# A hybrid two-layer trunk on one core: the causal mask moved into the scan, and elementwise steps of the attention half moved to GpSimd in quarter pieces

## The chip, the core and the metric

The kernel runs on one core of one Trainium2 chip. The metric is the device time in microseconds of one execution. The engines are TensorE (PE, with its weight loads as PEld), VectorE (DVE), ScalarE (ACT), GpSimd (POOL) and SyncE (SP, which issues most DMAs). Each engine runs its own instructions in order; they wait for each other through semaphores.

## The reference

All is float32; x is 2048 x 1024. Layer 0 is a pooling mixer, layer 1 a strictly causal stick-breaking attention over 16 heads of 64, with keys and values computed once between them:

```python
for i in range(DEPTH):                       # DEPTH = 2
    if i < N_A:                              # layer 0
        h = rms_norm(x, a_norm[i])
        x = x + pool_mixer(h, a_w_in[i], a_w_group[i], a_scale[i], a_w_out[i])
    else:                                    # layer 1
        k_all, v_all = jnp.split(rms_norm(x, kv_norm) @ w_kv, 2, axis=-1)
        k_sh, v_sh = rms_norm(split_heads(k_all), k_norm), split_heads(v_all)
        q, z = jnp.split(rms_norm(x, b_norm[j]) @ b_w_in[j], 2, axis=-1)
        q = rms_norm(split_heads(q), b_q_norm[j])
        o = stick_breaking_attention(q, k_sh, v_sh)
        x = x + (o * jax.nn.silu(z)) @ b_w_out[j]
    x = x + (p[i] @ ple_w[i]) * jax.nn.sigmoid(x @ ple_gate_w[i])

# attention: A[t,s] = beta[t,s] * prod_{s<j<t} (1 - beta[t,j]), beta = sigmoid(q.k / sqrt(d))
mask = s_idx < t_idx
log_keep = jnp.where(mask, jax.nn.log_sigmoid(-logits), 0.0)
later = lax.cumsum(log_keep, axis=log_keep.ndim - 1, reverse=True) - log_keep
a = jnp.where(mask, jnp.exp(jax.nn.log_sigmoid(logits) + later), 0.0)
out = a @ v
```

## The kernel before

The sequence is cut into four chunks of 512 rows (`W5`). Every float32 operand of a product is held as a pair, its high part and its low part (`pr[:, 0]`, `pr[:, 1]`), and a product is three matmuls: high x high, high x low, low x high. A layout with features on the partitions is used all through; a transpose is a matmul with the identity.

The first half of the program (a list of steps per chunk) computes layer 0, its embedding add and q, k and v, and leaves them in DRAM. The change touches there only the pool of the `halo` tiles.

The second half is the attention. Its main loop runs over passes n. A slot is a head h of query chunk c against key chunk kc (kc from c down to 0), and each slot has four passes, one for each block of 128 queries. Query chunks run from 3 to 0, so chunk 3 has 256 passes, chunk 2 192, chunk 1 128 and chunk 0 64. One pass issues, in this order:

- `turn` for the pass six earlier (L809 to L813): up to four transposes into a PSUM tile `psa` (two buffers), an ACT copy into the high part of `at` (L812), and a DVE subtraction for the low part (L813), which frees `psa`.
- `front` (L784 to L795): two matmuls make the logits in `psl` (two buffers), ACT writes `kap` = sigmoid(-logits) (L788, four tiles). In the diagonal slot (kc == c) a GpSimd select (L790) puts 1 wherever the key is not before the query in the last 128 columns. Then DVE scans backwards, a running product (multiply by `kap`, add zero), with the result of the slot before as the initial value (L795). Attention weights are differences of neighbouring running products; the differences are taken on v instead, in the first half.
- a number of filler matmuls: the generator `filler` yields after each matmul, and `rate` says how many a pass takes.
- `gather` for the pass eight earlier (L821, L822): two matmuls with `at` into `pso`. At the end of a head the two halves of `pso` are summed into `os` (ACT copy L826, DVE add L827). After every second head, four ACT instructions add a bias per query block (L833) and GpSimd multiplies by the gate of z (L834).

The filler of chunk 3 is `gate_z` (L883 to L886): for each of the four chunks, the product of z, the norm (a DVE multiply that reads PSUM), the sigmoid on ACT and the multiply on GpSimd, and a store. The filler of chunk c < 3 is `post(c+1)`: output projection and residual add (L907), the pair of the result `x3` (ACT cast L909, GpSimd subtraction L910), the gate product and its sigmoid (L929), the embedding product, a DVE multiply (L932), two last adds of the low and the high part of `x3` (L933 on GpSimd, on DVE in the tail; L934 on DVE), and in `finish` four transposes, an ACT copy into `ot` (one buffer) and the store (L939 to L942). `pair_up` makes the pair of an `os` (ACT cast L862, DVE subtraction L863). `post(0)` is the tail, after the loop; there `tail[0]` is set.

The order of instructions on each engine follows the order in which they are issued, with a scheduler that may move an instruction by a few places. What is left of a filler when a chunk of queries ends is issued at once; `rate` is the filler's number of steps over the passes that are to take it.

Of the kernel before, what the change touches and what calls it, by code (L numbers as in the profile page):

```python
# [8 lines left out]
F32 = mybir.dt.float32  # L9
# [25 lines left out]
def trunk_kernel(ctx, tc, x, p, a_norm, a_w_in, a_w_group, a_scale, a_w_out, kv_norm, w_kv,  # L35
# [143 lines left out]
    with ExitStack() as st:  # L179
# [17 lines left out]
        halo = [[cp.tile([P, HALO], F32, name=f"halo{o}_{i}") for i in range(2)] for o in range(KT)]  # L197
# [549 lines left out]
    with ExitStack() as st:  # L747
# [10 lines left out]
        V.memset(zeros, 0.0)  # L758
        kcount = [0]
# [17 lines left out]
        def front(st, j):  # L777

            w = (j + 1) * P if st["diag"] else W5
            r0 = W5 - w  # L780
            ps = psl.tile([P, W5], F32, tag="psl", name="psl")
            qs = slice(j * P, (j + 1) * P)
            (qa, qb), kk = st["q"], st["k"]
            T.matmul(ps[:, :w], qa[:, qs], kk[:, :w], start=True, stop=False)  # L784
            T.matmul(ps[:, :w], qb[:, qs], kk[:, :w], start=False, stop=True)  # L785
            kp = kaps[kcount[0] % NK]
            kcount[0] += 1
            A.activation(out=kp[:, r0:], in_=ps[:, :w], func=AF.Sigmoid, scale=-1.0)  # L788
            if st["diag"]:
                G.affine_select(out=kp[:, W5 - P :], in_=kp[:, W5 - P :], pattern=[[-1, P]], compare_op=ALU.is_gt,  # L790
                                fill=1.0, base=0, channel_multiplier=1)

            def scan():
                pp = ppool.tile([P, W5], F32, tag="pp", name="pp")
                V.tensor_tensor_scan(out=pp[:, r0:][:, ::-1], data0=kp[:, r0:][:, ::-1],  # L795
                                     data1=zeros.to_broadcast([P, w]),
                                     initial=1.0 if st["diag"] else st["carry"][j], op0=ALU.mult, op1=ALU.add)
                st["carry"][j] = pp[:, r0 : r0 + 1]
                st["a"].append((pp, r0))

            return scan
# [14 lines left out]
        def gather(st, kt):  # L816
# [6 lines left out]
            if st["last"] and kt == 3:  # L823
                half, os, c, h2 = st["h"] % 2, st["os"], st["c"], st["h"] // 2
                mine, other = slice(half * HD, (half + 1) * HD), slice((1 - half) * HD, (2 - half) * HD)
                A.copy(out=os[mine], in_=po[other])  # L826
                V.tensor_tensor(out=os[mine], in0=po[mine], in1=os[mine], op=ALU.add)  # L827
                if half:
# [5 lines left out]
                    G.tensor_tensor(out=os, in0=os, in1=zt, op=ALU.mult)  # L834
                    outs[c].append(os)

        tail = [0]
# [19 lines left out]
        def pair_up(c):  # L857

            if len(ogs[c]) < len(outs[c]):
# [3 lines left out]
                V.tensor_tensor(out=pr[:, 1], in0=os, in1=f(pr[:, 0]), op=ALU.subtract)  # L863
                ogs[c].append(pr)

        def gate_z(c):
# [11 lines left out]
            for o in range(KT):  # L878
# [4 lines left out]
                V.tensor_tensor(out=zr, in0=ps, in1=rb, op=ALU.mult)  # L883
                sg = t2.tile([P, W5], F32, tag="tmp", name="sgz", bufs=4)
                A.activation(out=sg, in_=zr, func=AF.Sigmoid)
                G.tensor_tensor(out=zr, in0=zr, in1=sg, op=ALU.mult)  # L886
# [5 lines left out]
        POST = 8 * 24 + 8 * 30 + 9  # L892

        def post(c):

            pin = t2.tile([P, 4, PLE], F32, tag="pin", name="pin", bufs=1)
# [4 lines left out]
            for o in range(KT):  # L901
# [8 lines left out]
                G.tensor_tensor(out=pr[:, 1], in0=xr, in1=f(pr[:, 0]), op=ALU.subtract)  # L910
# [12 lines left out]
            for o in range(KT):  # L923
                wg = stored(wgd[o])
                wl = stored(wld[o])
                ps = dense()
# [6 lines left out]
                (V if tail[0] else G).tensor_tensor(out=sg, in0=sg, in1=f(x3[o][:, 1]), op=ALU.add)  # L933
                V.tensor_tensor(out=sg, in0=sg, in1=f(x3[o][:, 0]), op=ALU.add)  # L934
# [14 lines left out]
                if c:  # L949
                    pair_up(c - 1)  # L950
                yield
# [25 lines left out]
        def begin(i):  # L977
            c, h, kc = slots[i]
            if kc == c:
                if h == 1:  # L980
                    early["ends"] = load_ends(c)
                os = head["os"] if h % 2 else t2.tile([P, W5], F32, tag="os", name="os", bufs=9)
                head.clear()
                head.update(q=early.pop("q", None) or load_q(c, h), carry=[None] * 4, o=[], os=os)
# [3 lines left out]
        for n in range(4 * len(slots) + LAG_G):  # L988
# [70 lines left out]
```

## Time and profile before

| | |
|---|---|
| time, median of 3 runs | 2778.84 us (2777.24 to 2779.99) |
| time of the profiled execution | 2781.82 us |
| its span, first to last instruction | 2779.0 us |
| PE busy | 2729.7 us (98%) |
| DVE busy | 1950.7 us (70%) |
| ACT busy | 1390.0 us (50%) |
| POOL busy | 956.8 us (34%) |
| DMA | 573.28 MB, mean 206 GB/s |
| mean granted TensorE clock | 0.999 |

The span ends some 3 us below the time of the same execution; what lies around it does not depend on the kernel's work. A row of a group names the source line, the engine, the operation, output <- inputs, the shape, the count, then busy us and mean ns of one, then the engine's idle time in front of it and what ended that. A row of the waits says who waited for whom: total us, times, longest. PE's matmuls overlap and their ends are modelled, so a busy PE isn't PE at its peak.

### The profile page before, as it was taken

What the parts mean: (1) busy time and instruction counts of PE and PEld (TensorE: products, weight loads), DVE (VectorE), ACT (ScalarE), POOL (GpSimd) and SP (SyncE); (2) the same over time, 40 slices, a digit from 0 to 9 for tenths busy, and PEclk for the clock granted to TensorE, in tenths of its full rate; (3) what the DMA queues carried; (4) which work ended last, traced back from release to release, by engine and by line L of the source; (5) the groups of instructions that cost most, each with busy time, mean ns of one, the idle gap of its engine ahead of it and who ended that gap; (6) DMA issues with size and microseconds to landing.
All of it is one profiled execution on the core that took longest, in us unless ns stands there. A gap on an engine that the chain in (4) does not pass through costs nothing. (4 is left out here: it accounts for less than half of the span.)

```text
span 2779.0 us, 40467 instructions
## 1 busy us (share of the span) xinstructions
PE 2729.7 (98%) x13715; PEld 2261.3 (81%) x13715; DVE 1950.7 (70%) x2573; ACT 1390.0 (50%) x2801; POOL 956.8 (34%) x949
## 2 busy tenths in 40 slices
PE   9999999999999999999999999999999999999999
PEld 7888888888888888888878888887878778878877
DVE  6667535655357544575499999999999988886642
ACT  5445532545234542345355566666666655564431
POOL 2575338642475425753211211121111122213220
PEclk9999999999999999999999999999999999999999
DMA  8655695737946488445688565555455655658765
GB/s 283 240 190 178 219 328 197 234 136 259 350 138 236 154 260 304 137 143 178 189 247 283 176 216 171 163 171 184 157 166 170 183 183 183 196 183 265 240 202 161
DMA packets 335844, 573.28 MB, mean 206 GB/s; under 512 B 32463, under 2 KB 166639, under 8 KB 335637
## 3 DMA queue, kind: packets, MB, share of 16 engines
q1 hardware_dynamic: 330186, 563.03, 62.3%
q10 hardware_dynamic: 5450, 7.66, 0.9%
q8 instruction: 108, 1.77, 0.3%
q14 instruction: 100, 0.81, 0.1%
HBM read 430.01 MB, written 132.19 MB: 202 GB/s over the span
## 5 line engine op out<-in xcount | busy, mean ns | idle before, releaser
L535 PE MATMUL psd<-wpair,x 128*128 128x512 f32 x2304 | 543.8, 393 | 0.0
L812 ACT CAST at<-psa 128x512 fp32r<-128x512 f32 (+3 forms) x640 | 333.4, 522 | 395.4 <-PE psa L809 389.4
L795 DVE TENSOR_TENSOR_SCAN pp<-kap,pp,zeros 128x512 f32<-128x512 f32 x384 | 507.6, 1323 | 6.2 <-ACT kap L788 4.8
L535 PEld LDWEIGHTS psd<-wpair,x 128*128 128x128 f32 x2304 | 428.1, 188 | 86.2
L813 DVE TENSOR_TENSOR at<-psa,at 128x512 fp32r<-128x512 f32 (+3 forms) x640 | 378.9, 594 | 58.1 <-ACT at L812 55.7
L809 PE MATMUL psa<-ident,pp 128*128 128x128 f32 x2176 | 346.4, 275 | 21.6 <-DVE at L813 17.7
L788 ACT ACTIVATE kap<-psl 128x512 f32<-128x512 f32 (+3 forms) x640 | 343.9, 538 | 18.9 <-PE psl L785 16.3
L809 PEld LDWEIGHTS psa<-ident,pp 128*128 128x128 f32 x2176 | 263.4, 140 | 99.4 <-DVE at L813 41.7
L790 POOL TENSOR_SCALAR_AFFINE_SELECT kap<-kap 128x128 f32<-128x128 f32 x256 | 93.2, 365 | 557.9 <-ACT kap L788 525.3
L784 PE MATMUL psl<-kk,qa 128*128 128x512 f32 (+3 forms) x640 | 280.6, 438 | 1.5 <-DMA kk<-kd 0.8
L795 DVE TENSOR_TENSOR_SCAN pp<-kap,zeros 128x128 f32<-128x128 f32 (+3 forms) x256 | 215.6, 842 | 43.3 <-POOL kap L790 39.6
L821 PE MATMUL pso<-at,vv 128*128 128x512 f32 (+3 forms) x640 | 234.5, 366 | 1.3 <-ACT at L812 1.2
L822 PE MATMUL pso<-at,vv 128*128 128x512 f32 (+3 forms) x640 | 235.4, 368 | 0.0
L785 PE MATMUL psl<-kk,qb 128*128 128x512 f32 (+3 forms) x640 | 234.1, 366 | 0.0
L131 PE MATMUL psd<-xp,wpair 128*128 128x512 f32 x512 | 202.0, 396 | 1.8 <-ACT xp L268 1.3
L132 PE MATMUL psd<-xp,wpair 128*128 128x512 f32 x512 | 200.7, 392 | 0.0
L133 PE MATMUL psd<-xp,wpair 128*128 128x512 f32 x512 | 200.1, 391 | 0.0
L113 DVE SCALAR_TENSOR_TENSOR wpair<-wraw,gains,wpair 128x512 fp32r<-128x512 f32 x192 | 170.6, 909 | 36.6 <-ACT wpair L112 33.2
L108 POOL TENSOR_TENSOR wpair<-wraw,wpair 128x512 fp32r<-128x512 f32 x99 | 144.4, 1475 | 60.4 <-ACT wpair L106 60.4
L112 ACT ACTIVATE wpair<-wraw,gains 128x512 fp32r<-128x512 f32 x192 | 135.0, 719 | 56.1 <-PE psd L535 32.0
L821 PEld LDWEIGHTS pso<-at,vv 128*128 128x128 f32 x640 | 120.4, 188 | 28.0 <-ACT at L812 2.3
L822 PEld LDWEIGHTS pso<-at,vv 128*128 128x128 f32 x640 | 120.4, 188 | 24.8
(210 smaller groups left out, 5453.9 us busy)
## 6 DMA issues: line engine op xcount, KB each, us to landing
kk<-kd SPq DMA_DIRECT2D x320, 128.0 KB
vv<-vd SPq DMA_DIRECT2D x160, 256.0 KB
wraw<-in_w_kv_dram SPq DMA_DIRECT2D x128, 256.0 KB
wpair<-wzd SPq DMA_DIRECT2D x64, 512.0 KB
wpair<-wod SPq DMA_DIRECT2D x64, 512.0 KB
wpair<-wgd SPq DMA_DIRECT2D x64, 512.0 KB
wpair<-wu SPq DMA_DIRECT2D x48, 512.0 KB
wpair<-wi SPq DMA_DIRECT2D x36, 512.0 KB
```

The source lines that it names most:

```text
L131: T.matmul(ps, wst(units, kt, 0, c0), acts[kt][:, 0], start=(begin and kt == order[0]), stop=False)
L132: T.matmul(ps, wst(units, kt, 0, c0), acts[kt][:, 1], start=False, stop=False)
L535: T.matmul(pss2[i], ck["x2"][kt][:, xh, tk], wst(ws, kt, wh, 0, W5), start=(kt == 0 and xh == 0 and wh == 0), stop=(kt == KT - 1 and wh == 1))
L784: T.matmul(ps[:, :w], qa[:, qs], kk[:, :w], start=True, stop=False)
L785: T.matmul(ps[:, :w], qb[:, qs], kk[:, :w], start=False, stop=True)
L788: A.activation(out=kp[:, r0:], in_=ps[:, :w], func=AF.Sigmoid, scale=-1.0)
L795: V.tensor_tensor_scan(out=pp[:, r0:][:, ::-1], data0=kp[:, r0:][:, ::-1], data1=zeros.to_broadcast([P, w]), initial=1.0 if st["diag"] els ...
L809: T.transpose(pt[:, j * P : (j + 1) * P], pp[:, r0 + kt * P : r0 + (kt + 1) * P], ident)
L812: A.copy(out=at[:, 0, cs], in_=pt[:, cs])
L813: V.tensor_tensor(out=at[:, 1, cs], in0=pt[:, cs], in1=f(at[:, 0, cs]), op=ALU.subtract)
L821: T.matmul(po[:, cs], vv[:, kt, :], at[:, 0, cs], start=(st["diag"] and kt == 0), stop=False)
L822: T.matmul(po[:, cs], vv[:, kt, :], at[:, 1, cs], start=False, stop=(st["last"] and kt == 3))
```

## The change

- The mask. A tile `ahead`, zero but for ones where the key is not before the query in the last 128 columns, is made once on GpSimd. In a diagonal slot the scan multiplies by `kap` and takes the maximum with `ahead`, and the select of `kap` on GpSimd is gone. Other slots scan as before.
- `pooled` runs an elementwise operation on GpSimd in four pieces of 128 columns; for the last pair of heads of chunk 0 and in the tail it is one DVE instruction.
- The head sum: ACT copies one half of `pso` into a new tile `low` and the other into `os`, and the sum is `pooled`. The multiply by the gate, the low part of an `os` (L863), the low part of `x3` and the two multiplies on z are `pooled` as well; for the norm of z ACT first copies the PSUM tile.
- The last sums: `xw`, the sum of both parts of `x3`, is made ahead of the gate product (`pooled`), and one add (`pooled`; DVE in the tail) takes the place of two.
- The filler of chunks 2 to 0 is spread over 64c - 4 passes in place of 64c - 16, and the last `finish` of a `post` is held back six steps (so `POST` is 448 and not 441).
- `halo` moves to a pool that ends with the first half, and `pin` is taken from the ring of pairs (18 buffers), which makes room for `ahead` and `low`.

```diff
@@ front
-            if st["diag"]:
-                G.affine_select(out=kp[:, W5 - P :], in_=kp[:, W5 - P :], pattern=[[-1, P]], compare_op=ALU.is_gt,
-                                fill=1.0, base=0, channel_multiplier=1)
...
-                V.tensor_tensor_scan(out=pp[:, r0:][:, ::-1], data0=kp[:, r0:][:, ::-1],
-                                     data1=zeros.to_broadcast([P, w]),
-                                     initial=1.0 if st["diag"] else st["carry"][j], op0=ALU.mult, op1=ALU.add)
+                if st["diag"]:
+                    V.tensor_tensor_scan(out=pp[:, r0:][:, ::-1], data0=kp[:, r0:][:, ::-1],
+                                         data1=ahead[:, r0:][:, ::-1], initial=1.0, op0=ALU.mult, op1=ALU.max)
+                else:
+                    V.tensor_tensor_scan(out=pp[:, ::-1], data0=kp[:, ::-1], data1=zeros.to_broadcast([P, W5]),
+                                         initial=st["carry"][j], op0=ALU.mult, op1=ALU.add)
@@ gather
-                A.copy(out=os[mine], in_=po[other])
-                V.tensor_tensor(out=os[mine], in0=po[mine], in1=os[mine], op=ALU.add)
+                low = st["low"]
+                last[0] = c == 0 and h2 == NH // 2 - 1
+                A.copy(out=low[mine], in_=po[other])
+                A.copy(out=os[mine], in_=po[mine])
+                pooled(os[mine], os[mine], low[mine], ALU.add)
...
-                    G.tensor_tensor(out=os, in0=os, in1=zt, op=ALU.mult)
+                    pooled(os, os, zt, ALU.mult)
+        def pooled(out, in0, in1, op):
+            if tail[0] or last[0]:
+                V.tensor_tensor(out=out, in0=in0, in1=in1, op=op)
+                return
+            for j in range(4):
+                js = slice(j * P, (j + 1) * P)
+                G.tensor_tensor(out=out[:, js], in0=in0[:, js], in1=in1[:, js], op=op)
@@ pair_up
-                V.tensor_tensor(out=pr[:, 1], in0=os, in1=f(pr[:, 0]), op=ALU.subtract)
+                pooled(pr[:, 1], os, f(pr[:, 0]), ALU.subtract)
@@ gate_z
-                V.tensor_tensor(out=zr, in0=ps, in1=rb, op=ALU.mult)
+                A.copy(out=zr, in_=ps)
+                pooled(zr, zr, rb, ALU.mult)
...
-                G.tensor_tensor(out=zr, in0=zr, in1=sg, op=ALU.mult)
+                pooled(zr, zr, sg, ALU.mult)
@@ post
-        POST = 8 * 24 + 8 * 30 + 9
+        POST = 8 * 24 + 8 * 31 + 8
...
-            pin = t2.tile([P, 4, PLE], F32, tag="pin", name="pin", bufs=1)
+            pin = f(pair("pin")).rearrange("q e (j n) -> q (e j) n", n=PLE)
...
-                G.tensor_tensor(out=pr[:, 1], in0=xr, in1=f(pr[:, 0]), op=ALU.subtract)
+                pooled(pr[:, 1], xr, f(pr[:, 0]), ALU.subtract)
...
+                xw = t2.tile([P, W5], F32, tag="tmp", name="xw", bufs=4)
+                pooled(xw, f(x3[o][:, 0]), f(x3[o][:, 1]), ALU.add)
...
-                (V if tail[0] else G).tensor_tensor(out=sg, in0=sg, in1=f(x3[o][:, 1]), op=ALU.add)
-                V.tensor_tensor(out=sg, in0=sg, in1=f(x3[o][:, 0]), op=ALU.add)
+                if tail[0]:
+                    V.tensor_tensor(out=sg, in0=sg, in1=xw, op=ALU.add)
+                else:
+                    pooled(sg, sg, xw, ALU.add)
...
+            for _ in range(6):
+                yield
             late.pop()()
@@ main loop
-                            rate = POST / (64.0 * c3 - 2 * LAG_G)
+                            rate = POST / (64.0 * c3 - 4)
```

More of the change, by code (lines that the diff above doesn't have):

```diff
@@ L195, in tmp @@
             return t2.tile([P, W5], F32, tag="tmp", name=nm, bufs=8)
-        halo = [[cp.tile([P, HALO], F32, name=f"halo{o}_{i}") for i in range(2)] for o in range(KT)]
+        hp = st.enter_context(tc.tile_pool(name="hp", bufs=1))
+        halo = [[hp.tile([P, HALO], F32, name=f"halo{o}_{i}") for i in range(2)] for o in range(KT)]
         for o in range(KT):
@@ L758, in trunk_kernel @@
         V.memset(zeros, 0.0)
+        ahead = kap.tile([P, W5], F32, name="ahead")
+        G.memset(ahead, 0.0)
+        G.affine_select(out=ahead[:, W5 - P :], in_=ahead[:, W5 - P :], pattern=[[-1, P]], compare_op=ALU.is_gt,
+                        fill=1.0, base=0, channel_multiplier=1)
         kcount = [0]
@@ L982, in begin @@
                 os = head["os"] if h % 2 else t2.tile([P, W5], F32, tag="os", name="os", bufs=9)
+                low = head["low"] if h % 2 else t2.tile([P, W5], F32, tag="low", name="low", bufs=1)
                 head.clear()
[L984 removed]
+                head.update(q=early.pop("q", None) or load_q(c, h), carry=[None] * 4, o=[], os=os, low=low)
             kk = early["k"].pop(0) if early["k"] else load_k(kc, h)
```

2 lines of the change are left out of this document (1 added, 1 removed).

## The prediction

> **What bounds the kernel now.** I read the page's busy times first, then the windows of the attention half cut at the four query chunks, then the waits of PE, DVE and ACT there, then groups and the timeline of single passes.
>
> ```profile
> PE 2729.7 (98%) x13715; PEld 2261.3 (81%) x13715; DVE 1950.7 (70%) x2573; ACT 1390.0 (50%) x2801; POOL 956.8 (34%) x949
> ```
>
> TensorE (PE) is nearly full over the whole span, VectorE (DVE) and the others are not. The windows below are chunks 3, 2, 1, 0 of the queries and the tail; the columns are length, busy time of PE, PE's weight loads, DVE, ACT and POOL, then clock and DMA.
>
> ```profile
> 1367.00:1868.00 501.00, 495.58 (x2695) 412.81 (x2694) 469.71 (x563) 299.54 (x597) 97.08 (x106) 1.00 0.65 204
> 1868.00:2225.00 357.00, 345.49 (x1919) 283.04 (x1917) 343.05 (x434) 227.83 (x468) 62.97 (x89) 1.00 0.55 172
> 2225.00:2488.00 263.00, 254.03 (x1399) 211.10 (x1399) 231.31 (x303) 157.23 (x337) 58.28 (x88) 1.00 0.60 188
> 2488.00:2662.00 174.00, 168.89 (x900) 141.90 (x901) 112.61 (x180) 87.28 (x206) 51.86 (x87) 0.99 0.77 247
> 2662.00:2779.00 117.00, 109.33 (x510) 88.93 (x508) 32.10 (x49) 24.01 (x47) 13.61 (x11) 0.98 0.52 167
> ```
>
> Length less PE busy is PE's idle time: 5.4, 11.5, 9.0, 5.1 and 7.7 us, together 38.7 us. The change issues the same matmuls, so this is the most that it can give back, though PE's ends are modelled and some waiting may hide in its busy time. DVE is at 94% and 96% in chunks 3 and 2, so there the two engines are close to a tie. The waits from 1367 to 2662 (total us, times, longest) say what holds DVE, and through it PE:
>
> ```profile
> PE psa L809 <- DVE at L813: 17.7, 33, 1.4
> ```
>
> ```profile
> DVE at L813 <- ACT at L812: 54.4, 113, 1.9
> DVE pp L795 <- POOL kap L790: 39.6, 62, 1.9
> DVE sg L934 <- POOL sg L933: 21.5, 18, 1.4
> ```
>
> ```profile
> ACT og L862 <- POOL os L834: 16.7, 15, 1.8
> ACT sgz L885 <- DVE zr L883: 13.4, 17, 2.6
> ```
>
> PE's largest wait is for DVE's subtraction, which frees the PSUM tile of the transposes; DVE itself waits 39.6 us for the mask on POOL and 21.5 us for the first of the two last sums.
>
> **The change part by part.** These are the groups in the same window (mean ns after the busy time):
>
> ```profile
> L795 DVE TENSOR_TENSOR_SCAN pp<-kap,pp,zeros 128x512 f32<-128x512 f32 x384 | 507.6, 1323 | 6.2 <-ACT kap L788 4.8
> L813 DVE TENSOR_TENSOR at<-psa,at 128x512 fp32r<-128x512 f32 x446 | 299.5, 672 | 35.3 <-ACT at L812 34.1
> ...
> L827 DVE TENSOR_TENSOR os<-pso,os 64x512 f32<-64x512 f32 x61 | 41.5, 680 | 4.9 <-ACT os L826 3.9
> ...
> L883 DVE TENSOR_TENSOR zr<-psd,rb 128x512 f32<-128x512 f32 x32 | 21.3, 667 | 0.4 <-PE psd L854 0.4
> L863 DVE TENSOR_TENSOR og<-os,og 128x512 fp32r<-128x512 f32 x30 | 21.3, 716 | 5.2 <-ACT og L862 5.2
> L934 DVE TENSOR_TENSOR sg<-sg,x 128x512 f32<-128x512 f32 x24 | 20.3, 846 | 21.5 <-POOL sg L933 21.5
> ```
>
> ```profile
> L790 POOL TENSOR_SCALAR_AFFINE_SELECT kap<-kap 128x128 f32<-128x128 f32 x256 | 93.2, 365 | 557.9 <-ACT kap L788 525.3 <-DVE pp L795 18.7 <-DVE at L813 8.9
> L886 POOL TENSOR_TENSOR zr<-zr,sgz 128x512 f32<-128x512 f32 x32 | 60.3, 1884 | 212.6 <-issue 136.7 <-ACT sgz L885 44.1 <-DVE at L813 19.5
> ```
>
> *DVE.* Head sums 62 x 0.680 = 42 us, norm of z 32 x 0.667 = 21, low parts of heads 31 x 0.716 = 22, last sums 24 x 0.846 = 20: 105 us of work leave DVE. The waits for the mask (39.6) and for POOL's half of the last sum (21.5) go too, 166 us in all out of the 1157 us that DVE is busy in the four chunks. What is late next behind the mask is the sigmoid on ACT, which the scan then waits for directly; behind the last sums it is nothing, since DVE no longer touches them.
>
> *The scan of the diagonal blocks* multiplies and takes the maximum instead of adding. No row shows that form; the nearest is the scan that adds, 1.323 us at full width. I have no reason for either sign, so I allow 3% both ways: 256 scans of at most 1.323 us make that at most 10 us of DVE time, inside the relief below, and I take 0. Making the `ahead` tile adds a memset and one select (nearest row 0.365 us) in front of the first scan, where four extra filler matmuls a pass cover it; uncovered it costs under 1 us.
>
> *POOL* loses 256 selects and runs some 260 operations in four pieces. The length of a piece is bounded by the select, 0.365, and by half of this one with 256 columns:
>
> ```profile
> L215 POOL TENSOR_TENSOR kpair<-kraw,kpair 128x256 fp32r<-128x256 f32 x8 | 6.4, 798 | 29.4 <-ACT kpair L214 29.4
> ```
>
> I take 0.40 us. What such pieces do to DVE is seen where a multiplication meets a scan, and the same rows give a pass of chunk 3:
>
> ```profile
> 1608.73 0.61 ACT L788 ACTIVATE kap<-psl 128x512 f32<-128x512 f32 x1
> ...
> 1609.47 1.28 DVE L795 TENSOR_TENSOR_SCAN pp<-kap,pp,zeros 128x512 f32<-128x512 f32 x1
> 1610.03 0.59 ACT L812 CAST at<-psa 128x512 fp32r<-128x512 f32 x1 [0.70 <-PE psa L809]
> 1610.51 0.60 ACT L788 ACTIVATE kap<-psl 128x512 f32<-128x512 f32 x1
> ...
> 1611.84 1.28 DVE L795 TENSOR_TENSOR_SCAN pp<-kap,pp,zeros 128x512 f32<-128x512 f32 x1
> ...
> 1612.13 2.08 POOL L886 TENSOR_TENSOR zr<-zr,sgz 128x512 f32<-128x512 f32 x1 [15.03 <-issue]
> ...
> 1613.35 0.69 DVE L813 TENSOR_TENSOR at<-psa,at 128x512 fp32r<-128x512 f32 x1 [0.23 <-ACT at L812]
> ...
> 1616.15 0.60 PE L809 MATMUL psa<-ident,pp 128*128 128x128 f32 x4
> ```
>
> The multiplication began 0.29 us into a scan and ended 1.09 us after it: it stood still for most of the scan, and ran beside the subtraction, which reads PSUM. So pieces run in the 0.69 us of a subtraction: two of 0.40 overrun it by 0.1, a burst of four needs two gaps and costs the scans some 0.2 us. 260 bursts x 0.2 = 52 us, if a scan gets its turn between pieces. That leaves 166 - 52 = 114 us of relief.
>
> The Trainium skill, in "SBUF — State Buffer", section "Who interferes with whom", says that a DVE instruction with two SBUF inputs and a GpSimd instruction that reads SBUF exclude one another for a whole instruction. By that rule a burst is delayed as in these rows, which agree with it.
>
> *ACT.* It gets 64 more copies of half heads and 32 of z. At the 0.59 us of the `at` copy in these rows that is 57 us; ACT is busy 300 of 501 us in chunk 3, so the time is there, and its order is the question. The changed program puts, in 18 of 32 cases, on ACT: copy of z, one `at` copy, sigmoid of z, sigmoid `kap`; in most others `kap` stands one place earlier. The sigmoid of z now waits for four POOL pieces, and `kap` or the next `at` is queued behind it, with DVE's scan and subtraction waiting for those. Worked on the pass above: `kap` ends at 1609.34, the copy of z fits into the 0.70 us hole, the scan bars POOL until 1610.75, four pieces end near 1612.35, the sigmoid (0.63) near 1613.0, `kap` near 1613.5 instead of 1611.11. The scan is late by 2.0 to 2.4 us. PE stands this for about 2.1 us: the subtraction that ended at 1614.04 freed the tile that the transposes took at 1616.15. So a z costs PE between 0 and 0.9 us (pieces of 0.365 or 0.47, scan early or late); I take 0.35, 32 x 0.35 = 11 us, and as DVE's backlog there otherwise goes (most of the 5.4 us), chunk 3 becomes 6 us longer. Before, DVE did this multiplication in 0.67 us and ACT lost 13.4 us in all.
>
> *Chunk 2.* Relief: 16 x 0.680 + 8 x 0.716 + 8 x 0.846 = 23 us, and about 10 + 7 of the two waits, against some 56 bursts x 0.2 = 11. DVE falls 29 us clear of PE, but eight pairs of heads make ACT wait for POOL (the 16.7 us row shows it now). Of 11.5 us idle I take 7 back.
>
> *Chunks 1 and 0.* The filler is now spread over 64c-4 passes instead of 64c-16. With c = 1, 441 steps in 48 passes become 448 in 60. Before, the last 16 passes of a chunk had no filler, and PE went at DVE's pace, 1.323 + 0.672 = 2.0 us a full pass. Of 9.0 and 5.1 us idle I take back 7 and 2.5.
>
> *Tail.* One sum fewer behind the last product:
>
> ```profile
> 2773.16 0.69 DVE L934 TENSOR_TENSOR sg<-sg,x 128x512 f32<-128x512 f32 x1
> ...
> 2775.12 0.59 ACT L941 COPY ot<-psao 128x512 f32<-128x512 f32 x1 [2.41 <-DMA out_dram<-ot]
> ```
>
> The last copy waits for the DMA of the tile before it, not for the sum, so the 0.69 us are hidden. I take 0. The first half of the program keeps its order. `pin` moves to another pool; its load is still issued eight products ahead of its use, cost 0.
>
> **Sum:** +6 - 7 - 7 - 2.5 = -10.5 us. The profiled execution took 2781.82 us, 3 above the median of 2778.84, so -10.5 against the median: 2768.
>
> **Rivals.**
> 1. *Slower: ACT's queue.* If the sigmoid of z runs more than 0.65 us later than worked above (each piece delayed by a scan of its own, or head sums queued behind z on POOL), every z costs PE 1.0 us: 32 - 5 = +27, and the pairs of heads halve the other gains to -8: +19, 2798. For it: ACT already waits in order for POOL and DVE (16.7 and 13.4 us). Against: DVE's lighter load lets it catch up between two z. It decides from a scan 2.1 us late on.
> 2. *No difference.* PE is the bound, chunk 3 loses about what chunks 2 to 0 win: 2777.
> 3. *Slower: the pieces hold the scans.* If each of the 640 scans waits for one piece, 640 x 0.40 = 256 us exceed the relief of 166 by 90, while DVE's free time in chunks 3 to 1 is 31 + 14 + 32 us; some 30 us come through, 2809. The Trainium skill, "Perfetto Trace Analysis", section "Optimizing Scalar/DVE Operations", warns that moving work between DVE and GpSimd might not help because they share a read port. Against: two pieces fit beside a subtraction.
>
> **How the numbers follow.** Forecast 0.50, rival 1 0.30, rival 2 0.12, rival 3 0.08. Both signs hold much, so the forecast's own range is 2750 to 2773: at best chunk 3 loses nothing and three quarters of the 38.7 us come back. The whole range takes in rivals 1 and 2, with 5 us for what the two prices of a piece leave open beyond rival 1 and 6 below for waiting hidden in PE's busy time: 2744 to 2803. About 0.2% (5.6 us) can be told from no change: faster 0.50, same 0.12, slower 0.38.
>
> **What would show it.** Right: PE's wait for the subtraction under 10 us in chunks 2 to 0, no DVE wait for POOL, DVE busy some 60 to 100 us less, and in chunk 3 a new ACT wait, sigmoid of z for POOL, of 1 to 2 us each. Rival 1: chunk 3 longer than 515 us. Rival 3: mean scan above 1.45 us. Wrong altogether: chunk 3 shorter than 495 us, or chunks 2 to 0 not shorter.

## The result, and the profile after

The changed kernel took 2815.65 us (median of 4 runs, 2814.37 to 2819.01) against 2778.04 for the kernel before beside it: a ratio of 1.0139, 95% interval 1.0126 to 1.0152. The forecast was 2768, the range 2744 to 2803; the time lies above both. The profiled execution took 2814.37 us, its span is 2812.5. From the page, section 1:

```profile
PE 2739.1 (97%) x13715; PEld 2266.9 (81%) x13715; DVE 1879.9 (67%) x2433; ACT 1435.8 (51%) x2897; POOL 1337.5 (48%) x1615
```

DVE has 71 us less work, as forecast (60 to 100), and the span is 33.5 us longer. So DVE's load did not decide. The same windows as before, cut at the chunks:

```profile
1366.00:1898.00 532.00, 503.82 (x2695) 413.37 (x2695) 438.77 (x510) 319.11 (x643) 254.09 (x369) 1.00 0.61 192
1898.00:2265.00 367.00, 347.17 (x1914) 285.72 (x1913) 332.20 (x402) 234.56 (x484) 157.80 (x228) 0.99 0.52 162
2265.00:2522.00 257.00, 252.23 (x1398) 210.73 (x1397) 214.10 (x275) 165.62 (x352) 130.17 (x220) 1.00 0.65 194
2522.00:2687.00 165.00, 162.18 (x881) 137.76 (x879) 101.96 (x147) 95.15 (x220) 111.72 (x212) 0.99 0.79 246
2687.00:2812.50 125.50, 117.03 (x537) 95.12 (x535) 35.70 (x54) 26.82 (x51) 8.00 (x17) 0.98 0.58 186
```

Chunk 3 grew by 31 us, chunk 2 by 9 to 10. Length less PE busy is 28.2, 19.8, 4.8, 2.8 and 8.5 us: PE idles 64.1 us where it idled 38.7, and is busy 9.1 us longer with the same matmuls (the last section shows where from). The last two windows must be read together: 881 and 537 matmuls stand where 900 and 510 stood, so filler went from chunk 0 into the tail. The waits from 1366 to 2687 say who waits:

```profile
DVE at L819 <- ACT at L818: 180.1, 235, 3.5
ACT sgz L905 <- POOL zr L854: 55.3, 30, 4.4
PE psa L815 <- DVE at L819: 35.4, 43, 3.4
DVE pp L802 <- ACT kap L794: 29.4, 32, 2.7
ACT os L842 <- POOL os L854: 23.6, 26, 2.5
ACT og L881 <- POOL os L854: 19.5, 16, 2.5
```

ACT now waits 98 us for GpSimd, in three places. Behind it DVE's wait for the high part of `at` rose from 54.4 to 180.1 us and PE's wait for the subtraction from 17.7 to 35.4. Of the two, PE's is the one to go by: the experiments will show DVE waiting nearly as long in a run that is 50 us faster. The timeline shows one such wait (start, length, then engine, line and tile; the bracket is the idle time before it):

```profile
1457.60 1.38 POOL L854 TENSOR_TENSOR os<-os,zt 128x128 f32<-128x128 f32 x1
...
1458.94 2.65 POOL L854 TENSOR_TENSOR zr<-zr,rb 128x128 f32<-128x128 f32 x4
1459.22 1.27 DVE L802 TENSOR_TENSOR_SCAN pp<-kap,pp,zeros 128x512 f32<-128x512 f32 x1
1459.36 0.66 PE L815 MATMUL psa<-ident,pp 128*128 128x128 f32 x4 [0.15 <-DVE at L819]
...
1460.08 0.39 PE L791 MATMUL psl<-kk,qb 128*128 128x512 f32 x1
...
1461.62 0.63 ACT L905 ACTIVATE sgz<-zr 128x512 f32<-128x512 f32 x1 [2.82 <-POOL zr L854]
1462.16 0.57 ACT L818 CAST at<-psa 128x512 fp32r<-128x512 f32 x1
...
1462.62 0.60 ACT L794 ACTIVATE kap<-psl 128x512 f32<-128x512 f32 x1
1462.76 0.69 DVE L819 TENSOR_TENSOR at<-psa,at 128x512 fp32r<-128x512 f32 x1 [2.27 <-ACT at L818]
...
1463.37 1.32 DVE L802 TENSOR_TENSOR_SCAN pp<-kap,pp,zeros 128x512 f32<-128x512 f32 x1
1463.50 0.66 PE L815 MATMUL psa<-ident,pp 128*128 128x128 f32 x4 [1.87 <-DVE at L819]
```

Four pieces of the norm of z took 2.65 us, as a scan came between them. They began only when GpSimd was done with the last piece of a gate's product, 1.1 us after ACT's copy of z had ended (at 1457.82). So the sigmoid of z stood at the head of ACT's queue for 2.82 us. Behind it stood the copy `at` of a transpose that PE had finished at 1460.02, and the sigmoid `kap` of logits finished at 1460.47. DVE had nothing for 2.27 us, and PE, whose PSUM tile DVE frees, for 1.87 us. This is one of the longer of these waits; 30 of them come to 55.3 us, 1.8 us each.

### The profile page after: what moved, and what is told of

The parts are those of the page before. It is cut to its first block, busy times and chain, and to the rows that moved or that the text cites. A ratio compares the mean times of both kernels' runs of the same rounds, so it can differ in the third digit from the quotient of the medians.

```text
span 2812.5 us, 40373 instructions
## 1 busy us (share of the span) xinstructions
PE 2739.1 (97%) x13715; PEld 2266.9 (81%) x13715; DVE 1879.9 (67%) x2433; ACT 1435.8 (51%) x2897; POOL 1337.5 (48%) x1615
## 5 line engine op out<-in xcount | busy, mean ns | idle before, releaser
L802 DVE TENSOR_TENSOR_SCAN pp<-kap,pp,zeros 128x512 f32<-128x512 f32 x384 | 510.6, 1330 | 31.4 <-ACT kap L794 29.4
L815 PE MATMUL psa<-ident,pp 128*128 128x128 f32 x2176 | 348.3, 275 | 43.3 <-DVE at L819 35.4
L854 POOL TENSOR_TENSOR os<-os,low 64x128 f32<-64x128 f32 x248 | 154.4, 651 | 236.9 <-ACT os L835 234.8
L799 DVE TENSOR_TENSOR_SCAN pp<-kap,ahead 128x128 f32<-128x128 f32 (+3 forms) x256 | 232.6, 909 | 18.1 <-ACT kap L794 16.8
L854 POOL TENSOR_TENSOR zr<-zr,rb 128x128 f32<-128x128 f32 x128 | 81.5, 665 | 204.7 <-ACT zr L902 204.7
L827 PEld LDWEIGHTS pso<-at,vv 128*128 128x128 f32 x640 | 120.7, 189 | 27.5 <-ACT at L818 0.5
```

Of the source, the lines that this page charges most:

```text
L802: V.tensor_tensor_scan(out=pp[:, ::-1], data0=kp[:, ::-1], data1=zeros.to_broadcast([P, W5]), initial=st["carry"][j], op0=ALU.mult, op1=AL ...
L815: T.transpose(pt[:, j * P : (j + 1) * P], pp[:, r0 + kt * P : r0 + (kt + 1) * P], ident)
L827: T.matmul(po[:, cs], vv[:, kt, :], at[:, 0, cs], start=(st["diag"] and kt == 0), stop=False)
L854: G.tensor_tensor(out=out[:, js], in0=in0[:, js], in1=in1[:, js], op=op)
```

## Experiments

Chunk lengths in this part run from the first sigmoid `kap` of one chunk to that of the next, in the profiled execution. "Theory Q" is the prediction's rival 1 taken further: the price is ACT waiting in order for GpSimd. "Theory P" is its rival 3: the pieces' own load on the port and on DVE. Each group of runs has its own runs of the kernel before; their medians went from 2778.1 to 2779.9. The first half of the program, which the edits leave as it is, ended 1364 to 1370 us into the profiled executions, so a few us between two runs can lie outside the attention.

**Two ways to take ACT's wait for z away.** First, issue the sigmoid later, all work staying on GpSimd:

```diff
-                sg = t2.tile([P, W5], F32, tag="tmp", name="sgz", bufs=4)
-                A.activation(out=sg, in_=zr, func=AF.Sigmoid)
-                pooled(zr, zr, sg, ALU.mult)
-                nc.sync.dma_start(out=zd[c][o], in_=zr)
+                zlate.append(silu)      # the four lines, issued nine filler steps on
```

> The changed kernel, with the same instructions, but the sigmoid of z and what follows it is issued nine filler steps (three to four passes) later, so that ScalarE does not reach it before GpSimd's four pieces are done. Theory Q (ScalarE's queue: sigmoid of z stands in front of the next kap and at copies while it waits for GpSimd): chunk 3 gives back about 25 of the 31 us that it lost, 2788 us (2780 to 2796), and the wait of the sigmoid of z for GpSimd, 55 us, falls under 5. Theory P (the pieces hold the scans through the shared port): the same pieces run, 2812 to 2818 us.

Second, the norm of z back on DVE:

```diff
-                A.copy(out=zr, in_=ps)
-                pooled(zr, zr, rb, ALU.mult)
+                V.tensor_tensor(out=zr, in0=ps, in1=rb, op=ALU.mult)
```

> The changed kernel with the norm of z back on VectorE, one instruction that reads PSUM, as before the change; nothing else. Theory Q: about 2790 us (2782 to 2798); VectorE gets 21 us of work back, ScalarE waits under 15 us for the norm. Theory P: 32 of some 260 bursts are gone, an eighth of the 37 us: 2811 us.

Measured: 2793.76 us (ratio to the kernel before 1.0049, 1.0034 to 1.0064) and 2794.37 (1.0053, 1.0036 to 1.0070). Chunk 3 fell from 533 to 511 and 509 us. The first of them still has every burst; what fell is the wait, in its waits over the attention:

```profile
PE psa L815 <- DVE at L819: 21.2, 27, 3.4
...
ACT sgz L912 <- POOL zr L854: 4.4, 3, 1.7
```

So 22 us of the 37.6 were z's, by Q. The remaining 16 us lay in neither theory's number.

**One GpSimd instruction in place of four pieces**, in the changed kernel:

```diff
-            for j in range(4):
-                js = slice(j * P, (j + 1) * P)
-                G.tensor_tensor(out=out[:, js], in0=in0[:, js], in1=in1[:, js], op=op)
+            G.tensor_tensor(out=out, in0=in0, in1=in1, op=op)
```

> The changed kernel with each step on GpSimd as one instruction of 512 columns instead of four of 128. Theory Q: 1.28 us in one lock instead of four times 0.455 us with up to two scans in between, so ScalarE waits less: 2802 us (2795 to 2810). Theory P: a whole instruction holds a waiting scan longer than a piece: 2825 us or more, mean scan above 1.40 us.

Measured: 2800.51 us (1.0073, 1.0057 to 1.0088), 15 us faster than in pieces. Its groups, against the changed kernel's 1330 ns for the same scan, and its waits:

```profile
L802 DVE TENSOR_TENSOR_SCAN pp<-kap,pp,zeros 128x512 f32<-128x512 f32 x384 | 557.2, 1452 | 17.4 <-ACT kap L794 16.0
```

```profile
ACT sgz L903 <- POOL zr L852: 24.7, 29, 1.7
```

```profile
L852 POOL TENSOR_TENSOR zr<-zr,rb 128x512 f32<-128x512 f32 x32 | 53.2, 1663 | 265.4 <-ACT zr L900 265.4
```

This is the plainest row against theory P. Whole instructions do hold the scans, as it expected: 0.12 us each on average or 47 us in all. Yet the kernel is faster, as ACT waits 24.7 us for z in place of 55.3. The norm of a z is ready sooner: in 1.66 us, where in the changed kernel's trace its four pieces, with scans between them, take 2.55 us on average from the first's start to the last's end. The quarter pieces spare DVE at the price of ACT's wait.

**The parts that gain, one by one.** The mask alone on the kernel before; then the new spread of the filler; on top of both the last sums; on top of both the low parts; and all four together:

```diff
 mask:       select of `kap` gone, scan of diagonal slots by `ahead` and max, `halo` and `pin` moved
 spread:     rate = POST / (64.0 * c3 - 4), POST = 8 * 24 + 8 * 31 + 8, six empty steps
 last sums:  pooled(xw, x3 high, x3 low, add) ahead, pooled(sg, sg, xw, add) behind
 low parts:  pooled(pr[:, 1], os or xr, f(pr[:, 0]), ALU.subtract)
```

> The kernel before with the mask in the scan alone (ahead tile, maximum, halo and pin in other pools); no step goes to GpSimd. Both theories: VectorE's 39.6 us of waits for the select go, and about a third of that reaches PE: 2768 us (2760 to 2776). If instead the scan with the maximum and a full second operand is slower by over 5%, the 256 diagonal scans' mean rises from 0.84 us and the time stays at 2778 or above.

> The kernel before with the mask in the scan (2773) and only the new spread of the filler: 448 steps over 64c-4 passes, six empty steps ahead of the last output tile. Prediction's step: chunks 1 and 0 get back most of their idle time, so 2768 (2763 to 2771), chunk 1 near 258 and chunk 0 near 163, with some 6 us of filler moved from chunk 0 into the tail. Rival: the filler that is now left at the end of a chunk falls upon the first passes of the next and costs what it gains: 2772 to 2778, chunk 2 longer than 358.

> The run with mask and spread, and the last sums in quarter pieces on GpSimd as in the change (the sum of the two parts of x3 ahead, then one addition): 24 x 0.85 us leave DVE, 48 bursts come. In the run with z put back PE waits some 7 us in chunk 2 for output transposes whose sum is late on GpSimd. Theory Q: PE's queue is held, 4 to 8 us slower than the run with mask and spread alone. Rival, the prediction's step: DVE relief of 20 us and of the wait for the first sum, 2 to 5 us faster than it.

> The run with mask and spread, and the low parts of heads (from DVE) and of x3 (from one GpSimd instruction) in quarter pieces on GpSimd. Nobody on ACT waits for these. Theory Q: within 3 us of the run with mask and spread alone, sooner faster than slower. Theory P: 56 bursts with 224 pieces between scans cost 4 to 8 us.

> The kernel before with those parts of the change that gained alone: mask in the scan, the new spread, last sums and low parts in quarter pieces; the norm of z, head sums and the two products stay as before. If the gains add (mask 7, spread 2, last sums 10, low parts 11 us under 2779): 2750, between 2744 and 2756; PE idle under 10 us from the first scan to the last. Rival: last sums and low parts both win the same idle time of PE, so the second adds little: 2757 to 2764. Beside the run without head sums and z (2766), which is this one with the two products in quarter pieces too, it also gives the price of those pieces.

| | us | ratio to the kernel before (interval) |
|---|---|---|
| mask | 2772.63 | 0.9972 (0.9961 to 0.9983) |
| mask, spread | 2771.07 | 0.9969 (0.9957 to 0.9980) |
| mask, spread, last sums | 2761.21 | 0.9936 (0.9919 to 0.9952) |
| mask, spread, low parts | 2760.06 | 0.9935 (0.9920 to 0.9950) |
| all four | 2751.97 | 0.9903 (0.9888 to 0.9918) |

Here the prediction's idea holds: work leaves DVE in pieces, no engine waits long in order for the result, and PE gets idle time back. The spread by itself is not told from no change (1.6 us, the intervals overlap). Theory Q's expectation that the last sums hold PE's queue was wrong: they gain 10 us. The low parts gain 11, more than Q (within 3) and against P (a loss). All four together run 27 us faster than the kernel before; the gains nearly add, and this version beats both kernels. The windows of that run, chunks 3 and 2:

```profile
1365.10:1862.50 497.40, 495.50 (x2704) 414.00 (x2703) 469.51 (x557) 298.27 (x599) 103.01 (x71) 1.00 0.66 206
1862.50:2211.30 348.80, 341.87 (x1907) 282.65 (x1906) 336.54 (x418) 225.23 (x467) 107.25 (x133) 1.00 0.56 170
```

PE idles 1.9 and 6.9 us there. DVE is busy 469.5 us in chunk 3, as much as before the change (469.7), and PE is nearly full all the same.

**Head sums.** The changed kernel with both z and head sums as before, so that mask, spread, low parts, last sums and the two products (z by its sigmoid, heads by their gate) are left in pieces; and one with the two copies on ACT kept, but the sum on DVE:

```diff
-                A.copy(out=low[mine], in_=po[other])
-                A.copy(out=os[mine], in_=po[mine])
-                pooled(os[mine], os[mine], low[mine], ALU.add)
+                A.copy(out=os[mine], in_=po[other])                                # first run
+                V.tensor_tensor(out=os[mine], in0=po[mine], in1=os[mine], op=ALU.add)
+                V.tensor_tensor(out=os[mine], in0=os[mine], in1=low[mine], op=ALU.add)  # second run, after both copies
```

> The changed kernel with the norm of z and now also the head sums on DVE as before (62 copies of half heads and 62 bursts less on top of the run with z alone put back, 2794). Theory Q, ACT's order: ACT waits for the head sums in the biases (8.5 and 11.2 us in chunks 3 and 2 of that run), and what is queued behind comes late; so chunk 3 returns to 500-503 us (from 509) and chunk 2 loses some 5 of its 367: 2781, between 2775 and 2787. Theory P, every burst of quarter pieces costs its DVE time wherever its result is awaited: 62 of some 250 bursts left, so a quarter of the 17 us that remain above the kernel before's 2778: 2790, between 2787 and 2794.

> The changed kernel with the norm of z on DVE, and of the head sums the two copies on ACT as changed but the sum on DVE in one instruction. What it has over the run without z and head sums (2766) is one more half copy on ACT a head; what it lacks against the run with z alone put back (2794) are the bursts and ACT's wait for them. Theory Q: 2768, between 2764 and 2774. Rival, ACT's extra copy holds the logits' sigmoids back and is the price: 2782 to 2794.

Measured: 2765.61 us (0.9952, 0.9937 to 0.9967) and 2765.36 (0.9954, 0.9939 to 0.9968). Head sums on GpSimd cost 28.8 us (2794.37 less 2765.61), more than either theory gave, and ACT's second copy costs nothing. So it is the burst, or the wait for it. To tell these apart, the changed kernel with everything on GpSimd and two of the three things that wait on ACT issued late (the third, the cast `og` behind the gate's product, stays where it was): the sigmoid of z as above, and the four biases of a pair of heads one a pass, from three passes after the sum on:

```diff
-                        A.activation(out=os[:, js], in_=os[:, js], func=AF.Identity, bias=ends[c][:, h2, j : j + 1])
-                    pooled(os, os, zt, ALU.mult)
+                        hlate.append(lambda js=slice(j * P, (j + 1) * P): bias(js))
+                    hlate.append(gate)     # the loop over n pops one a pass
```

> The changed kernel with everything on GpSimd, but what ACT waits for issued later: sigmoid of z nine filler steps later as before (2794), and the four biases of a pair of heads one a pass, from three passes after their sum was put on GpSimd on, the gate's product behind them. Theory Q, ACT waiting in order is the price of the head sums too: most of the 29 us that they cost (2794 against 2766) come back, 2771, between 2764 and 2780. Rival: the price is the two copies of each head on ACT or the bursts themselves, which stay: 2786 to 2796.

Measured: 2765.22 us (0.9954, 0.9937 to 0.9971). The whole change, every piece of it, with two groups of instructions issued later, is 50 us faster than the changed kernel and 13 us faster than the kernel before. Its waits, to be read against 180.1, 19.5, 35.4, 23.6 and 55.3 above:

```profile
DVE at L819 <- ACT at L818: 163.0, 267, 2.8
ACT og L896 <- POOL os L863: 27.1, 17, 2.8
PE psa L815 <- DVE at L819: 10.1, 16, 1.1
ACT os L842 <- POOL os L863: 8.0, 9, 2.2
ACT sgz L927 <- POOL zr L863: 3.2, 3, 1.7
```

The two waits that were to go are gone, and with them PE's. DVE still waits for `at` about as long as in the changed kernel (163.9 us from 1366 to 2645 there), so that wait is not the price.

**Is late issue a gain by itself?** The four gaining parts, norm of z and head sums on DVE, sigmoid and biases late; beside it all on GpSimd and late, with the two products whole; and the four parts with either product in pieces:

```diff
 four parts, late:    zlate and hlate as above, norm and sums on DVE, products whole
 all late, whole:     pooled(zr, zr, sg, ...) and pooled(os, os, zt, ...) -> G.tensor_tensor(...)
 product of z:        G.tensor_tensor(out=zr, in0=zr, in1=sg, ...) -> pooled(zr, zr, sg, ...)
 product of the gate: G.tensor_tensor(out=os, in0=os, in1=zt, ...) -> pooled(os, os, zt, ...)
```

> The run with the four gaining parts (2752), norm of z and head sums on DVE and the products whole as there, but sigmoid of z and biases issued as late as in the run with all late. It tells whether late issue is a gain by itself: then the 22 and 28 us that it won for the changed kernel do not show that waiting for GpSimd was the price. Theory Q: DVE makes these in 0.7 us and ACT lost 14 us in all to them, so 0 to 6 us faster: 2745 to 2753. Rival, lateness helps whoever makes the operand: 10 us or more faster, 2742 or less.

> The run with all late (2765) with the two products, of z with its sigmoid and of a pair of heads with its gate, as one GpSimd instruction each in place of four. It now differs from the run with the four gaining parts only in the norm of z and the head sums on GpSimd, with late issue. If the quarter products cost what lies between 2766 and 2752: 2752, between 2748 and 2757, so the two moves off DVE are then worth nothing, even where nobody waits for them. Rival: the quarter products cost only where ACT waits, so no difference here: 2761 to 2768.

> The run with the four gaining parts (2752) with the product of z and its sigmoid in quarter pieces: 96 more instructions on GpSimd, in chunk 3 alone. If quarter products are the 13.6 us between that run and 2766: chunk 3 8 us longer, 2760, between 2756 and 2764. Rival, that difference came from the order of instructions ahead of the attention (the first scan 4.5 us later there): within 3 us of 2752.

> The run with the four gaining parts (2752) with the product of a pair of heads and its gate in quarter pieces. ACT's copy into the low-part pair is the next reader. If quarter products are the 13.6 us: 4 to 6 us, mostly in chunk 2 (353 us in place of 349): 2757, between 2754 and 2761. Rival, as for the product of z: within 3 us of 2752.

| | us | ratio (interval) |
|---|---|---|
| four parts, late | 2751.15 | 0.9901 (0.9887 to 0.9916) |
| all late, whole products | 2765.05 | 0.9954 (0.9937 to 0.9970) |
| four parts, product of z in pieces | 2756.87 | 0.9923 (0.9907 to 0.9940) |
| four parts, product of the gate in pieces | 2764.12 | 0.9948 (0.9933 to 0.9963) |

Late issue wins nothing where DVE makes the operand (2751.15 against 2751.97), so what it won for the changed kernel was the wait for GpSimd. With all late, whole products win nothing either (2765.05 against 2765.22), where 2752 had been expected. The product of the gate in pieces costs 12 us, more than was expected (2757), 9 of them in chunk 2 (357.5 against 348.8). The product of z in pieces costs 5 us by the medians, but its profiled execution is only 2 us longer in chunk 3, the one chunk that has z, where 8 were expected; 6 lie in chunk 0 and the tail, where two stretches of 3.4 us at half clock (the last section) make 3.4 of them, as an estimate. So a price of that product is not shown. The next reader of the gate's product is a cast on ACT (`og`), so theory Q says the same once more. The last runs try that, with the cast issued six passes or more after the product, and try what is left in the run with all late:

```diff
 gate late:  if c: pair_up(c - 1)  ->  want.append(c - 1), served by the loop over n six passes after the product or later
 sums on DVE, all late:  pooled(os[mine], os[mine], low[mine], ...) -> V.tensor_tensor(...)
```

> The run with the gate's product in quarter pieces (2764), with the cast of its result on ACT (the high part of the pair) issued six passes or more after the product, and the casts spread evenly. Theory Q: the price of 12 us is ACT waiting in order for the product (24 us there against 16), so it comes back: within 4 us of the run of this group with the whole product. Rival: the price is the pieces between the scans: 8 us or more above it.

> The run with the four gaining parts (2752), product of the gate as one instruction, with the cast issued as late as in the run beside it. ACT waited 16 us for that product there: 2746 to 2752, and the base for the quarter pieces with a late cast.

> The run with all late (2765), with the sum of the two half heads, after the same two copies on ACT, made by DVE in one instruction. The run with late issue and both moves undone took 2751; 14 us are left of the two moves though nobody waits long for them. Theory S: what is left are the bursts of the head sums, behind which the scans were held 2.3 to 4.6 us in five places (9.5 us over their own 1.27): 2755, between 2751 and 2760, and no scan longer than 1.7 us. Rival: it is the work that the moves put on ACT, or the norm of z: 2761 to 2767.

Measured: with pieces and late cast 2753.09 us (0.9907, 0.9892 to 0.9921), with the whole product and late cast 2754.66 (0.9908, 0.9892 to 0.9925). No difference: with the cast late the pieces cost nothing, so the 12 us came from the cast's early place in ACT's queue. The whole product did not gain from a late cast (2746 to 2752 had been expected). The row in the waits of the run with pieces and the early cast, then in the one with the late cast:

```profile
ACT og L876 <- POOL os L849: 24.4, 17, 2.4
```

```profile
ACT og L877 <- POOL os L850: 5.1, 4, 2.1
```

The sum of such a wait is not its price, though. In the run with four parts late ACT waited as long for the same product, and the time was 2751.15:

```profile
ACT og L895 <- POOL os L845: 25.0, 20, 3.0
```

So it must depend on what is queued behind the waiting instruction, which these runs don't take apart further.

The sums on DVE with all late took 2763.26 us (0.9941, 0.9926 to 0.9955), 2 below the run with the sums in pieces. The long scans did go (the longest took 1.96 us, with the sums in pieces 4.60), so theory S, that the bursts of the head sums hold the scans for those 14 us, falls. What costs 12 to 14 us when norm of z and head sums are on GpSimd, or copied by ACT, and nobody waits long for them, stays open. Two copies without lateness cost nothing (2765.36 against 2765.61), and z late on GpSimd took the same as z on DVE (2793.76 against 2794.37). One rival was not run: the cast `og` was early in all of these, and still waited 24 to 27 us.

## Why the prediction was wrong

Rival 1 came true, and more of it. Working back from the runs: four gaining parts -26.6 us (2778.6 to 2752.0), products in pieces +13.6 (to 2765.6), head sums +28.8 (to 2794.4), norm of z +21.3 (to 2815.7). They come to +37.1, and +37.6 was measured. The split holds for this order of steps alone: with everything issued late the products in pieces cost nothing. Step by step:

- *What bounds.* Right for PE: of its 38.7 us of idle time some 18 are left in the run with all four gaining parts. Its busy time is 10 us shorter there too, the waiting that the prediction said might hide in it. But "DVE is close to a tie" was read as "DVE is what to relieve": that run keeps DVE as busy in chunk 3 as before, and the changed kernel relieved DVE by 31 us there and lost 31.
- *The norm of z.* This is the first term that failed. ACT's wait came as forecast (1 to 2 us each, 1.8 measured); what was mis-sized is how much of it reaches PE: 0.35 us for each z, 11 us in all. The two runs that undo it give 22.5 and 24 us in chunk 3, 0.70 to 0.76 each. Two of its numbers were off. Pieces were taken as 0.40 us, and a burst in the worked pass as 1.6 us; undisturbed four take 1.69 to 1.72 us (the rows at 2162.85 and 2164.53 below), with a scan between them 2.65, and the 32 of z took 2.55 on average. And PE was said to stand a scan 2.1 us late, from one pass in which only `kap` stood behind the sigmoid. In the rows above an `at` stands behind it too: the scan starts 4.15 us after the one before it, where full passes before the change lay 2.37 us apart (1609.47 and 1611.84), so 1.8 us later than that, and PE idles 1.87.
- *Head sums.* The second and larger failure is a sign. Their 42 us were counted as relief and their wait, "eight pairs of heads make ACT wait for POOL", was named and not priced in the sum. It cost 28.8 us. The sum's chunk 2, -7, became +9: DVE did fall clear of PE there (332 of 367 us) and it did not help.
- *The products.* Going from one instruction to four pieces was left at nothing in the sum; beside the four gaining parts it costs 13.6 us, most of it by the `og` cast queued early behind the gate's product (12 us with that product alone in pieces, gone with the cast late). The row of 16.7 us before the change was this wait.
- *Mask, last sums, low parts.* Right in kind: with the spread these parts won 27 us. The scan of the diagonal blocks was allowed 3% either way, 10 us at most, and taken at 0, which holds for the form itself. The groups by shape, first of the kernel before, then of the run with the mask alone:

```profile
L795 DVE TENSOR_TENSOR_SCAN pp<-kap,zeros 128x512 f32<-128x512 f32 x64 | 79.1, 1235 | 10.8 <-POOL kap L790 10.4
...
L795 DVE TENSOR_TENSOR_SCAN pp<-kap,zeros 128x256 f32<-128x256 f32 x64 | 46.9, 734 | 20.1 <-POOL kap L790 20.0
```

```profile
L799 DVE TENSOR_TENSOR_SCAN pp<-kap,ahead 128x512 f32<-128x512 f32 x64 | 79.5, 1243 | 1.3 <-ACT kap L794 1.2
...
L799 DVE TENSOR_TENSOR_SCAN pp<-kap,ahead 128x256 f32<-128x256 f32 x64 | 54.8, 856 | 2.5 <-ACT kap L794 2.1
```

  At full width it is as long as before (1243 against 1235 ns). At 256 columns the mean is 17% longer, but not by the form: the median is 680 ns (691 before), and 16 of the 64 scans are held, most of them beside a GpSimd multiplication of 512 columns, by the gate or the sigmoid of z. With these in pieces (the first run under head sums above) the same form takes 729 ns. The idle time ahead of it, for the select, is gone. Mask alone won 7 us.
- *Chunks 1, 0 and the tail.* Forecast -7 and -2.5. Chunk 1 won 5.5, and 3.5 by the spread alone; chunk 0 and tail together took 288.9 us where they had taken 288.5. The spread counts 60 passes for chunk 0, but a filler starts when the last `gather` of the chunk before is done, eight passes into the 64, so 4 x 448/60 = 30 steps are left for the tail: 27 matmuls more in its window.
- *Rival 3.* Its test, a mean scan above 1.45 us, did not come: 1330 ns after, 1323 before. By the Trainium skill, "Perfetto Trace Analysis", section "Optimizing Scalar/DVE Operations", moving work between DVE and GpSimd might not help for the port they share. Here last sums and low parts moved so did help (10 and 11 us), and where the move did not, a queue on ACT was most of the reason; 12 to 14 us stay unexplained.
- *Rival 1* had the mechanism and the place, and chunk 3 passed its 515 us. Its 2798 was too low because it let the pairs of heads only halve other gains; its 1.0 us for a z was above the 0.70 to 0.76 measured.

## What to carry to other kernels

When a step moves to a slower engine, look at who reads its result, and at what is queued in order behind that reader: here DVE's load fell, and the time went into a third engine that waited. A result that no in-order queue needs soon can move for gain (last sums, low parts); one that is read at once moves only together with its reader, issued some passes later. Splitting an instruction so that others may come between its pieces makes its own result late, and paid here only where nobody waited for that.

## What the hardware showed that was not expected

*A run of GpSimd pieces can hold a scan off for longer than any one instruction.* Mostly pieces give way: one of them stretches to 1.4 us while the scan keeps its 1.27. But in eight places of the changed kernel's trace a scan took 2.26 us or more, seven times behind pieces of a head sum and once behind those of a low part, with pieces of other operations queued right behind. The longest, in the timeline:

```profile
2162.85 1.72 POOL L854 TENSOR_TENSOR os<-os,low 64x128 f32<-64x128 f32 x4 [12.23 <-ACT os L835]
...
2163.76 4.37 DVE L802 TENSOR_TENSOR_SCAN pp<-kap,pp,zeros 128x512 f32<-128x512 f32 x1
...
2164.53 1.69 POOL L854 TENSOR_TENSOR sg<-sg,xw 128x128 f32<-128x128 f32 x4
...
2166.18 3.56 POOL L854 TENSOR_TENSOR xw<-x 128x128 f32<-128x128 f32 x4
...
2168.36 0.66 PE L815 MATMUL psa<-ident,pp 128*128 128x128 f32 x4 [3.37 <-DVE at L819]
```

Ten of the twelve pieces ran with no break between them (1.72 and 1.69 us for the first two groups of four), the scan was done 4.37 us after its start, and only the last two pieces had to wait for scans. The Trainium skill, "SBUF — State Buffer", section "Who interferes with whom", has the two exclude one another for a whole instruction; this trace agrees, and adds that the turn need not change after one instruction. Five of the eight are scans of full width; these lost 8.5 us over their 1.27 us in sum. With whole instructions the mean full-width scan rose to 1452 ns.

*A pause of PE of some 2 us can be followed by 3.4 us at half clock.* The granted clock is the number behind POOL's in the windows:

```profile
1758.00:1763.40 5.40, 3.56 (x14) 2.98 (x14) 4.75 (x5) 1.84 (x4) 4.66 (x7) 0.68 0.07 25
1763.50:1768.00 4.50, 4.50 (x27) 3.79 (x26) 3.01 (x5) 2.58 (x6) 0.00 (x0) 1.00 0.66 213
```

PE's timeline of that place, after a pause of 1.86 us and then at full clock again:

```profile
1761.17 0.63 PE L871 MATMUL psd<-xz,wpair 128*128 128x512 f32 x1
1761.60 0.63 PE L873 MATMUL psd<-xz,wpair 128*128 128x512 f32 x1
...
1764.11 0.40 PE L871 MATMUL psd<-xz,wpair 128*128 128x512 f32 x1
1764.34 0.39 PE L873 MATMUL psd<-xz,wpair 128*128 128x512 f32 x1
```

The same matmuls start 0.43 us apart in place of 0.23. From the first scan to 30 us before its end the changed kernel's trace has five such stretches of 3.4 us, that of the kernel before one, that of the run with four gaining parts none, and that with the gate's product in pieces four, so some of its 12 us are these. In the changed kernel four more at half of 3.4 us are, as an estimate, 7 of the 9.1 us by which PE's busy time grew. Pauses of up to 2.4 us elsewhere (at 1390) had no such stretch behind them. The five stretches begin on one grid: their starts lie 46, 74, 106 and 52 times 3.413 us apart. In four of the five grid intervals just ahead of them PE idles 1.9 to 2.5 us, in the fifth 1.5. The pause at 1390 falls across two intervals, with at most 1.7 us in one. That orders them roughly; no single limit comes out, as intervals with 1.6 and 1.7 us had no stretch behind them. By the Trainium skill, "TensorE: Matmul & The Clock Gate", Part 1, the clock falls after an idle window of about 3.4 us; here pauses of 1.5 to 2.1 us were enough four times.
